# Attention stage: where the queue of GpSimd begins the reload of x, the value chunks and the z gates

## The chip, the cores and the metric

The kernel runs on one core of one Trainium2 chip. A core has TensorE (PE, matrix multiply), VectorE (DVE), ScalarE (ACT), GpSimd (POOL) and SyncE (SP). Each engine works through its own instructions in order, and engines wait for each other on semaphores. SP, ACT and POOL also begin DMA transfers; all transfers of the core share 16 DMA engines. The metric is the device time of one execution in microseconds (us), the median of several runs.

## The reference

One layer of an encoder with 2048 tokens (a grid of 32 rows by 64 columns) and 1024 features. What matters here:

```python
h = rmsnorm(x, norm_w) * (1 + scale) + shift
proj = h @ w_in + b_in              # q, k, v, z of 8 attention heads; inputs of 4 mLSTM heads
na_out = neighbourhood_attention(na_q, na_k, na_v, rpb) * silu(na_z)   # window of 8 rows by 16 columns
ml_out = groupnorm(mlstm_forward + mlstm_backward, gated) * silu(ml_z)
y = concatenate([na_out, ml_out]) @ w_out
x = x + gate * y
out = rmsnorm(x, final_norm_w)
```

All inputs and the output are float32.

## The kernel before, in words

Phase 1 computes the projections and the mLSTM branch. Phase 2, the part that the change touches, is the neighbourhood attention, the output projection, the residual and the final norm. It begins at about 1005 us of the span.

**Patches, units, slots.** The 2048 queries are cut into 16 patches of 128 (8 grid rows by 16 columns). A patch has four units of two heads each. A *slot* (`slot(m)`) takes the two units of its number (`new`) through scores and softmax and the two of the slot before (`old`) through the values. So each patch has a **first slot** (m even) and a **second slot** (m odd); a slot takes about 10 to 11 us. In a slot PE first does the scores of the new units (L1341), then the values of the old ones (L1384), then four groups of transposes of the new probabilities (`turned`, L1369, n = 0 to 3). Between these groups `pump` puts matmuls of the output projection (L1429) of an earlier patch, so that PE has work while DVE and ACT do the softmax. Where DVE is late with a softmax, PE stands at the next transpose, since its order is fixed when the program is written.

**Softmax.** DVE adds the table of biases (`tab`) to the scores and takes a minimum (L1349), ACT takes the exponential (L1350), DVE normalises (L1361). Tables are loaded by SP (`load_tab`, L1313), where the next unit that needs another one follows: issued in one slot, right behind the exponential that read the old table, and read at the start of the next slot.

**What POOL does here.** In phase 2 POOL computes almost nothing; it begins DMA transfers, strictly in program order, and a transfer whose semaphores are not there yet holds up all behind it:

- value chunks `v` of the next patch (L1269), six buffers; each waits until PE has read the buffer's last chunk. They are begun by `loads(n)`: the unit with i = 1 of a patch begins one, the unit with i = 2 one, the unit with i = 3 the rest;
- the z gates of the next patch (L1279, tiles `zs` and `gtile` in turn), begun by `loads(n)` at i = 2; they wait until DVE has split the gated output that lies in that tile (L1404);
- the mLSTM half of the mixed rows (L1286, `load_m`, tiles `whi_a` and `wlo_a`);
- the store of a finished patch (L1472), which waits for DVE's last multiply (L1471);
- the reload of the rows of x (L1297, `load_x`) for the patch after the next one, 512 KB into the buffer that the store has just read. It waits for that store to land. The rows are needed where DVE adds the projection to x (L1434).

**When a store and a reload are called.** `step()` is called behind the second and the fourth group of transposes of each slot and takes one entry of the list `todo`. The store puts two entries behind itself:

```python
nc.gpsimd.dma_start(to, x)
if nxt not in (None, last_b):
    self.todo += [lambda: None, lambda: load_x(nxt)]
```

The store comes behind the fourth group of a second slot; so the empty entry is taken at the next step, behind the second group of the first slot of the next patch, and the reload behind its fourth group. In front of all groups of a slot stands `for n in new: loads(n)`. That POOL gets to these instructions early or late is decided by their semaphores and by what stands ahead of them in POOL's order, not by PE's place in the slot.

Of the kernel before, what the change touches and what calls it, by code (L numbers as in the profile page):

```python
# [62 lines left out]
class Kernel:  # L63
# [1142 lines left out]
    def phase2(self):  # L1206
# [45 lines left out]
        def load_q(i):  # L1252
            if 2 * i >= NU:
                return
            b, c0 = units[2 * i][0], min(units[2 * i][1], units[2 * i + 1][1])
            (nc.gpsimd, nc.gpsimd, nc.scalar, nc.sync)[min(i, 3)].dma_start(qs[i % 3].bitcast(F32), self.d_qna[:, c0 // 2, b].rearrange("e p c q -> p e c q"))

        def load_v(b, most=4, queue=nc.gpsimd):

            pr, pc, nr, nkc, nk, rpc, nch = geo[b]  # L1260
            up = pc % 2 == 0
            for i in reversed(range(nch)) if up else range(nch):
                r0 = PR_R0[pr] + i * rpc
                key = (pc, r0) if nkc == 32 else (b, r0)
                if key not in chunks and most:
                    most -= 1
                    n = rpc if nkc == 32 else min(rpc, nr - i * rpc)
                    chunks[key] = p.tile([P, 512], F32, tag="v", bufs=6, name=f"v_{b}_{i}")
                    queue.dma_start(chunks[key][: n * nkc, :], vg[r0 : r0 + n, PC_C0[pc] : PC_C0[pc] + nkc, :])  # L1269
            L[b]["v"] = [  # L1270
                (chunks.get(((pc if nkc == 32 else b), PR_R0[pr] + i * rpc)), min(rpc, nr - i * rpc) * nkc) for i in range(nch)
            ]
# [5 lines left out]
        def load_z(b, queue=nc.gpsimd):  # L1278
            queue.dma_start(zs[pos[b] % 2], self.d_zna[b])  # L1279
# [8 lines left out]
        def load_x(b):  # L1288
            pr, pc = divmod(b, 4)
            src = xg[8 * pr : 8 * pr + 8, 16 * pc : 16 * pc + 16, :]  # L1290
            if b == last_b:
                L[b]["x"] = [p.tile([P, 512], F32, tag="v", bufs=6, name=f"xr_{b}_{i}") for i in range(2)]
                for i, x in enumerate(L[b]["x"]):
                    nc.gpsimd.dma_start(x, src[:, :, 512 * i : 512 * i + 512])
                return
            x = flat(self.raw.tile([P, 4, 256], F32, tag=f"raw{pos[b] % 2}", name=f"xr_{b}"))
            nc.gpsimd.dma_start(x, src)  # L1297
            L[b]["x"] = [x[:, 512 * i : 512 * i + 512] for i in range(2)]
            L[b]["row"] = x
# [56 lines left out]
        def normalised(u):  # L1356
            nk = geo[units[u][0]][4]
            pts, sums = U[u]
            nc.vector.reciprocal(sums, sums)
            for j in range(2):  # L1360
                nc.vector.tensor_scalar(pts[j][:, :nk], pts[j][:, :nk], sums[:, j : j + 1], None, ALU.mult)  # L1361
            U[u] = pts
# [11 lines left out]
        def values(pair):  # L1374
            po = pO.tile([P, 2, P], F32, tag="pO", name=f"pO_{pair[0]}")
            for u in pair:
                b, ct = units[u]
                nch = geo[b][6]
                pt = U.pop(u)
                for i in range(nch):  # L1380
                    v, n = L[b]["v"][i]
                    for j in range(2):
                        h = 2 * ct + j
                        nc.tensor.matmul(po[j * HD : (j + 1) * HD, ct % 2, :], v[:n, h * HD : (h + 1) * HD], pt[j][:n, i, :], start=(i == 0), stop=(i == nch - 1))  # L1384
            return po
# [12 lines left out]
        def mix_high(b, half):  # L1398
            nc.scalar.activation(mix_parts(b)[0][:, 4 * half : 4 * half + 4, :], mix_source(b, half), AF.Copy)  # L1399

        def mix_low(b, half):
            split.add((b, half))
            hi, lo = (part[:, 4 * half : 4 * half + 4, :] for part in mix_parts(b))
            nc.vector.tensor_tensor(lo, mix_source(b, half), hi.bitcast(F32), ALU.subtract)  # L1404

        def outproj(b):
# [9 lines left out]
            nxt = after.get(after.get(b))  # L1416
# [52 lines left out]
            def store():  # L1469
                x = lb["row"]  # L1470
                nc.vector.scalar_tensor_tensor(x, x, rst, fnw[0].bitcast(F32), ALU.mult, ALU.mult)  # L1471
                nc.gpsimd.dma_start(to, x)  # L1472
                if nxt not in (None, last_b):
                    self.todo += [lambda: None, lambda: load_x(nxt)]

            if end:
                self.between.append(scale)
# [34 lines left out]
        def loads(n):  # L1512
            b, ct = units[n]
            i = n % 4
            nb = after.get(b)
            if b == last_b and i == 1:
                load_x(b)
            if nb is not None and i:
                load_v(nb, 1 if i < 3 else 4)
                if i == 2 and b != b0:  # L1520
                    load_z(nb)

        self.flush()
        while self.left > 108 or self.jobs:
            self.pump(3)
            self.job()
            self.flush()
        self.between, self.squares = [], []

        def step():  # L1530
            if self.between:
# [7 lines left out]
        def mixed(b, half):  # L1539
            mix_high(b, half)  # L1540
            mix_low(b, half)
            if half:
                self.queue.append(outproj(b))

        def slot(m):
            new = (2 * m, 2 * m + 1) if 2 * m < NU else ()
            old = (2 * m - 2, 2 * m - 1) if m else ()
            if m:
                load_q(m + 2)
            if new:  # L1550
                scores(new)
            if old:
                po = values(old)
            if new:
                normalised(new[0])
            if old:
                gated(old, po)
            if new:
                normalised(new[1])
            b = units[old[0]][0] if m > 2 and old[0] % 4 == 2 else None  # L1560
            for n in new:
                loads(n)
            if not new:
                mixed(b, 1)
                mixed(b, 0)
                for _ in range(2):
                    self.pump(12)
                    finish()
                    step()
                return  # L1570
            fills = [8, 7, 7, 7, 7] if m < 3 else [6, 5, 5, 4, 4]
            for n in range(-1, 4):
                if n >= 0:
                    turned(new[n // 2], n % 2)
                    if n % 2:
                        step()
                    finish()
                    if n in (1, 2) and b is not None:
                        mixed(b, n % 2)
                for fn in extra.pop((m, n), ()):  # L1580
                    fn()
                self.pump(fills[n + 1])
            if m == 2:
                self.pump(max(0, self.left) + 1)
                self.owed = 0
                mixed(b0, 1)
                mixed(b0, 0)
# [90 lines left out]
```

## Time and profile before

| what | number |
|---|---|
| time, median of 3 runs (lowest, highest) | 1388.98 us (1385.2 to 1394.62) |
| the profiled execution's own time | 1390.2 us |
| its span (first to last instruction) | 1388.4 us |
| PE busy | 1299.3 us, 94% of the span |
| DVE / ACT / POOL busy | 792.7 / 531.3 / 284.5 us |
| mean granted TensorE clock of the profiled execution | 0.981 of full speed |
| DMA queues, share of 16 engines over the span: SP's / POOL's / ACT's | 48.7% / 11.0% / 9.9% |
| store of a patch from issue to landing, 512 KB, 15 times | 6.8 us median |
| reload of x from issue to landing, 512 KB, 15 times | 9.4 us median |

How to read it: the rows of a timeline give an instruction's start in us from the start of the span, its duration, the engine, the line of the kernel, the operation, the tiles (written <- read), and in brackets how long the engine stood idle before it and what ended that. "DMA share" is the part of the 16 DMA engines' time in which they moved packets. q0 is the queue of the transfers that POOL begins, q1 that of SP's.

### The profile page before, as it was taken

Reading aid. Unit: us, or ns where it says so; the run is one execution under the profiler, and the core shown is the slowest. Engines: PE = TensorE matmul, PEld = TensorE weight load, DVE = VectorE, ACT = ScalarE, POOL = GpSimd, SP = SyncE. Lnnn points to the kernel's source line nnn. Section 1 sums busy time; section 2 is a strip of 40 time slices with the busy share of each in tenths; the row PEclk is TensorE's granted clock in tenths of the full one; section 3 lists DMA queues with packets and bytes.
Section 4 is the critical chain, followed back from the end, with each engine's and each line's share of the span. In section 5 each row is a group of like instructions: output and inputs, shape, how many; then the busy total and the mean of one; then the engine's idle time right before and its main releaser. Section 6 shows DMA issues by size and latency. Waiting matters only on the chain.

```text
span 1388.4 us, 23353 instructions
## 1 busy us (share of the span) xinstructions
PE 1299.3 (94%) x8204; PEld 1111.8 (80%) x8204; DVE 792.7 (57%) x2428; ACT 531.3 (38%) x1123; POOL 284.5 (20%) x306
## 2 busy tenths in 40 slices
PE   3989998998999999999999998999999999899996
PEld 2989998998887777888878876778877777778775
DVE  6683423211355569246767876867737666657664
ACT  4642334523222223213323322323346555555552
POOL 4453222424101010001213001212202211111121
PEclk9999999999999999999999999899999999999998
DMA  9799448768457685554676787646689986666971
GB/s 327 226 296 209 123 116 222 199 189 200 121 115 206 148 192 159 163 168 139 190 215 203 233 238 259 178 135 180 174 255 248 206 214 180 174 173 175 211 180 46
DMA packets 243271, 263.28 MB, mean 190 GB/s; under 512 B 31814, under 2 KB 200006, under 8 KB 243154
## 3 DMA queue, kind: packets, MB, share of 16 engines
q1 hardware_dynamic: 151774, 186.18, 48.7%
q0 software_dynamic: 20496, 36.21, 11.0%
q10 hardware_dynamic: 70884, 39.40, 9.9%
q8 instruction: 65, 1.06, 0.3%
q14 instruction: 52, 0.43, 0.1%
HBM read 177.18 MB, written 92.72 MB: 194 GB/s over the span
## 4 chain that ended last, share of the span: by engine, by line
PE 46%; DMA 9%; DVE 5%; issue 3%; ACT 1%; POOL 1%; ACTq 0%; SPq 0%; DVEq 0%; POOLq 0%
PE pq L866 18%; PE y L1429 10%; DMA tab<-d_t 4%; PE pT L1369 3%; PE pO L1384 3%; DMA kv<-d_ck 2%; PE pS L1341 2%; PE pc L430 2%; PE pc L429 2%; PE pc L431 2%; PE pi L1090 2%; PE px L1088 1%; PE dc L1036 1%; DVE pbuf L1349 1%; DMA d_mix<-zt 1%
## 5 line engine op out<-in xcount | busy, mean ns | idle before, releaser
L866 PE MATMUL pq<-hhi,whi_a 128*128 128x512 f32 x512 | 208.5, 407 | 1.9 <-DVE qst L901 1.1
L866 PE MATMUL pq<-hlo,whi_a 128*128 128x512 f32 x512 | 208.7, 408 | 0.0
L866 PE MATMUL pq<-hhi,wlo_a 128*128 128x512 f32 x512 | 208.1, 406 | 0.0
L866 PEld LDWEIGHTS pq<-hhi,whi_a 128*128 128x128 f32 x512 | 97.2, 190 | 19.5 <-issue 1.5
L866 PEld LDWEIGHTS pq<-hhi,wlo_a 128*128 128x128 f32 x512 | 97.3, 190 | 16.6
L866 PEld LDWEIGHTS pq<-hlo,whi_a 128*128 128x128 f32 x512 | 97.1, 190 | 16.7 <-issue 0.5
L1371 ACT ACTIVATE pt<-pT 96x384 f32<-96x384 f32 (+3 forms) x128 | 65.9, 515 | 85.9 <-PE pT L1369 82.7
L1350 ACT ACTIVATE pbuf<-pbuf,mn 128x480 f32<-128x480 f32 (+5 forms) x128 | 76.1, 596 | 57.3 <-DVE mn L1349 57.1
L1429 PE MATMUL y<-hhi,wlo_a 128*128 128x512 f32 (+1 forms) x272 | 91.4, 402 | 0.2 <-ACT y L1436 0.2
L1429 PE MATMUL y<-hhi,whi_a 128*128 128x512 f32 x256 | 90.6, 415 | 0.5 <-ACT whi_a L1399 0.5
L1349 DVE CUSTOM_DVE_ANT_0 pbuf<-pS,tab 128x480 f32<-128x480 f32 (+5 forms) x128 | 63.1, 539 | 45.6 <-PE pS L1341 33.6
L840 POOL TENSOR_TENSOR wlo_a<-rawq,whi_a 128x1024 fp32r<-128x1024 f32 x20 | 48.4, 2420 | 170.5 <-ACT whi_a L839 145.2
L429 PE MATMUL pvo<-whi_b,hhi 128*128 128x256 f32 x256 | 75.5, 295 | 5.7 <-DVE stvo L499 5.7
L1112 POOL TENSOR_TENSOR hm<-hm,ck 128x128 f32<-128x128 f32 x64 | 26.4, 412 | 259.5 <-DVE hm L1111 184.8
L1369 PE MATMUL pT<-ident,pbuf 128*128 128x128 f32 (+2 forms) x416 | 67.4, 275 | 12.2 <-DVE pbuf L1361 10.5
L1369 PEld LDWEIGHTS pT<-ident,pbuf 128*128 128x128 f32 (+2 forms) x416 | 50.6, 137 | 34.7 <-issue 14.5
L1093 ACT ACTIVATE num<-px,gtile 128x129 f32<-128x129 f32 x120 | 38.2, 365 | 104.9 <-PE px L1088 85.9
L431 PE MATMUL pvo<-whi_b,hlo 128*128 128x256 f32 x256 | 74.3, 290 | 0.0
L430 PE MATMUL pvo<-wlo_b,hhi 128*128 128x256 f32 x256 | 74.2, 290 | 0.0
L1020 DVE TENSOR_SCALAR wv<-kv,gtile 128x129 f32<-128x129 f32 x120 | 37.7, 322 | 62.5 <-DMA kv<-d_ck 31.8
L714 ACT ACTIVATE dec<-dec,gtile 128x128 f32<-128x128 f32 x128 | 42.0, 392 | 71.4 <-POOL dec L710 62.3
L499 DVE TENSOR_TENSOR stvo<-pvo,brow 128x256 f32<-128x256 f32 x64 | 26.5, 420 | 74.9 <-PE pvo L431 61.0
(295 smaller groups left out, 3447.5 us busy)
## 6 DMA issues: line engine op xcount, KB each, us to landing
ck<-d_ck SPq DMA_DIRECT2D x64, 384.5 KB
kv<-d_ck SPq DMA_DIRECT2D x120, 128.5 KB
rawq<-in_w_main_dram SPq DMA_DIRECT2D x28, 512.0 KB
raw<-in_w_main_dram SPq DMA_DIRECT2D x20, 512.0 KB
d_ck<-stvo SPq DMA_DIRECT2D x16, 514.0 KB
x<-in_x_dram SPq DMA_DIRECT2D x16, 512.0 KB
wada<-in_w_ada_dram SPq DMA_DIRECT2D x32, 256.0 KB
dec<-d_mneg SPq DMA_DIRECT2D x32, 256.0 KB
```

Source lines behind the costliest of these rows:

```text
L429: nc.tensor.matmul(ps, lhi(k), rhi(k), start=(k == 0), stop=False)
L430: nc.tensor.matmul(ps, lhi(k), rlo(k), start=False, stop=False)
L431: nc.tensor.matmul(ps, llo(k), rhi(k), start=False, stop=(k == KT - 1))
L714: nc.scalar.activation(t[:, d, o, :], t[:, d, o, :], AF.Exp, bias=self.cols["g"][:, d, h, c : c + 1])
L840: nc.gpsimd.tensor_tensor(lo[:, :, cs], raw, hi[:, :, cs].bitcast(F32), ALU.subtract)
L866: nc.tensor.matmul(patch_ps(ps) if patch else ps, w, self.htok(h, g, k, patch), start=(k == 0 and n == 0), stop=(k == KT - 1 and n == 2))
L1349: nc.vector.tensor_tensor_reduce(pt[:, :nk], ps, tabs[place[u]][j][:, :nk], 1.0, 3e38, ALU.add, ALU.min, mn)
L1350: nc.scalar.activation(pt[:, :nk], pt[:, :nk], AF.Exp, bias=mn, scale=-1.0, accum_out=sums[:, j : j + 1])
L1369: nc.tensor.transpose(ps[:cs, i, :], U[u][j][:, i * cs : (i + 1) * cs], self.ident)
L1371: nc.scalar.activation(t[:cs, :nch, :], ps[:cs, :nch, :], AF.Copy)
L1384: nc.tensor.matmul(po[j * HD : (j + 1) * HD, ct % 2, :], v[:n, h * HD : (h + 1) * HD], pt[j][:n, i, :], start=(i == 0), stop=(i == nch - 1))
L1429: nc.tensor.matmul(y, m[:, k, :], w[k][:, cs], start=(k == 4 and n == 0), stop=(k == 3 and n == 2))
```

## The change

Two things. The reload of x gets a list of its own, `reloads`, of which one entry is taken in every slot, behind the second group of transposes; its two entries (the empty one and the reload) are therefore taken in two slots that follow each other. And `loads` of the two new units are called behind the first and the third group of transposes, not in front of all groups.

```diff
@@ store(), in outproj
                 nc.gpsimd.dma_start(to, x)
                 if nxt not in (None, last_b):
-                    self.todo += [lambda: None, lambda: load_x(nxt)]
+                    self.reloads += [lambda: None, lambda: load_x(nxt)]
@@
-        self.between, self.squares = [], []
+        self.between, self.squares, self.reloads = [], [], []
@@ slot(m)
             b = units[old[0]][0] if m > 2 and old[0] % 4 == 2 else None
-            for n in new:
-                loads(n)
             if not new:
@@
                     finish()
                     if n in (1, 2) and b is not None:
                         mixed(b, n % 2)
+                    if n in (0, 2):
+                        loads(new[n // 2])
+                    if n == 1 and self.reloads:
+                        self.reloads.pop(0)()
                 for fn in extra.pop((m, n), ()):
                     fn()
```

The order of instructions on PE, DVE, ACT and SP stays as it was, row for row; only POOL's order changes. In the steady part it looks as follows, on POOL before, from the store of one patch to the store of the next (`xr` is a patch's rows of x, the number behind a name only tells buffers apart):

```order
L1472 DMA out_dram<-xr_11866 8x16x1024
L1269 DMA v_1_12303<-d_vna 128x1x512
L1286 DMA whi_a<-d_mix 128x512
L1297 DMA xr_12356<-in_x_dram 128x1x1024
L1269 DMA v_0_12418<-d_vna 128x1x512
L1279 DMA gtile<-d_zna 128x512
L1472 DMA out_dram<-xr_12117 8x16x1024
```

The same place on POOL in the changed kernel:

```order
L1472 DMA out_dram<-xr_11973 8x16x1024
L1286 DMA whi_a<-d_mix 128x512
L1269 DMA v_1_12344<-d_vna 128x1x512
L1269 DMA v_0_12433<-d_vna 128x1x512
L1279 DMA gtile<-d_zna 128x512
L1297 DMA xr_12459<-in_x_dram 128x1x1024
L1472 DMA out_dram<-xr_12216 8x16x1024
```

The mixed rows (L1286) have moved from behind the first value chunk to ahead of it, the second value chunk now directly follows the first, and the reload of x (L1297) has moved past the second value chunk and past the z gates.

At the start of phase 2, on POOL before (`hlo` are the output weights):

```order
L1269 DMA v_2_10566<-d_vna 120x1x512
L1316 DMA hlo_105<-d_wo 128x1024
L1297 DMA xr_10621<-in_x_dram 128x1x1024
L1316 DMA hlo_105<-d_wo 128x1024 x3
L1269 DMA v_1_10707<-d_vna 120x1x512
L1279 DMA zs<-d_zna 128x512
L1269 DMA v_0_10710<-d_vna 120x1x512
L1286 DMA wlo_a<-d_mix 128x512
L1297 DMA xr_10756<-in_x_dram 128x1x1024
```

And there in the changed kernel:

```order
L1316 DMA hlo_105<-d_wo 128x1024
L1269 DMA v_2_10617<-d_vna 120x1x512
L1297 DMA xr_10621<-in_x_dram 128x1x1024
L1316 DMA hlo_105<-d_wo 128x1024 x3
L1286 DMA wlo_a<-d_mix 128x512
L1269 DMA v_1_10722<-d_vna 120x1x512
L1279 DMA zs<-d_zna 128x512
L1269 DMA v_0_10752<-d_vna 120x1x512
L1297 DMA xr_10756<-in_x_dram 128x1x1024
```

Here one value chunk has moved behind the first load of output weights, and the mixed rows ahead of three other loads. The first two reloads of x (which `extra` calls, not `reloads`) stay where they were.

## The prediction

> **What bounds the kernel now.** I read the page's head first, then the busy time by stretch, then PE's waits, then the chain of work that ended last.
>
> ```profile
> span 1388.4 us, 23353 instructions
> PE 1299.3 (94%) x8204; PEld 1111.8 (80%) x8204; DVE 792.7 (57%) x2428; ACT 531.3 (38%) x1123; POOL 284.5 (20%) x306
> ```
>
> PE is the bound over the whole span; the change touches the attention stage alone. The next rows give its stretches (us from the start; length; busy time and instructions of PE, PE's weight loads, DVE, ACT and POOL; granted clock, DMA share, GB/s).
>
> ```profile
> 1084.00:1128.00 44.00, 40.45 (x298) 31.70 (x297) 25.96 (x91) 22.82 (x62) 8.42 (x14) 1.00 0.93 208
> 1128.00:1193.00 65.00, 65.00 (x494) 51.52 (x492) 42.99 (x136) 36.60 (x91) 11.75 (x19) 1.00 0.66 178
> 1193.00:1214.00 21.00, 17.09 (x120) 13.54 (x117) 12.83 (x45) 10.35 (x28) 3.15 (x5) 0.92 0.86 206
> 1281.00:1350.00 69.00, 68.09 (x508) 53.61 (x506) 44.20 (x153) 38.54 (x106) 15.50 (x25) 1.00 0.85 195
> ```
>
> Where the DMA engines are 66% busy PE has no gap at all; it loses time only where they are at 85% or more. What it loses, and to whom, between 1084 and 1350 us, where the change acts:
>
> ```profile
> PE pT L1369 <- DVE pbuf L1361: 8.4, 7, 3.9
> ```
>
> Seven waits, 8.4 us, each a transpose that stands for a softmax. The chain of work that ended last tells why DVE was late (start, length, what; the lines between are PE's):
>
> ```profile
> 1090.06 9.21 DMA tab<-d_t
> ...
> 1110.30 11.10 DMA tab<-d_t
> ...
> 1196.08 12.51 DMA tab<-d_t
> ```
>
> Three times the chain leaves PE for a load of a bias table. All three are issued in a first slot and read at the start of the second slot, that is, in the stretch in which POOL's queue also holds the store, a value chunk, the mixed rows, the reload of x and another chunk. Five of PE's seven waits stand in second slots:
>
> ```profile
> 1100.50 0.51 PE L1369 MATMUL pT<-ident,pbuf 128*96 128x128 f32 x3 [1.08 <-DVE pbuf L1361]
> ...
> 1122.76 0.41 PE L1369 MATMUL pT<-ident,pbuf 128*128 128x128 f32 x2 [2.12 <-DVE pbuf L1361]
> ...
> 1210.00 0.88 PE L1369 MATMUL pT<-ident,pbuf 128*128 128x128 f32 x3 [3.91 <-DVE pbuf L1361]
> ...
> 1213.26 0.71 PE L1429 MATMUL y<-hhi,wlo_a 128*128 128x512 f32 x2
> ...
> 1334.18 0.51 PE L1369 MATMUL pT<-ident,pbuf 128*120 128x128 f32 x3 [0.27 <-DVE pbuf L1361]
> ```
>
> With one of 0.45 us between the last two shown, the five sum to 1.08 + 2.12 + 3.91 + 0.45 + 0.27 = 7.83 us; the two in first slots have the rest of the 8.4, 0.6 us. The longest costs more than itself: the granted clock of its stretch is 0.92, and from the first transpose after it to the matmul behind the second group of transposes PE takes 1213.26 - 1210.00 = 3.26 us. The same sequence without a wait:
>
> ```profile
> 1186.35 0.49 PE L1369 MATMUL pT<-ident,pbuf 128*128 128x128 f32 x3
> ...
> 1188.07 0.48 PE L1429 MATMUL y<-hhi,whi_a 128*128 128x512 f32 x1
> ```
>
> takes 1.72 us, so the slower clock adds 1.5 us. **The ceiling of what the change can give is 7.8 + 1.5 = 9.3 us, 0.7%**. A measurement of this kernel can tell about 1% (14 us) from no change.
>
> **The change, part by part.** No instruction is added or removed, and PE, DVE, ACT and SP keep their order. Only POOL's order of transfers changes, and POOL computes nothing here until the last patch; so every term is a transfer that starts earlier or later, worth what it does to a waiting reader or to the 16 DMA engines. POOL's timeline of one patch:
>
> ```profile
> 1191.23 0.62 POOL L1472 DMA_DIRECT2D out_dram<-xr  x1 [5.54 <-DVE xr L1471]
> 1194.62 0.68 POOL L1269 DMA_DIRECT2D v<-d_vna  x1 [2.77 <-PE pO L1384]
> 1195.28 0.61 POOL L1286 DMA_DIRECT2D whi_a<-d_mix  x1
> 1198.25 0.60 POOL L1297 DMA_DIRECT2D xr<-in_x_dram  x1 [2.36 <-issue]
> 1198.85 0.68 POOL L1269 DMA_DIRECT2D v<-d_vna  x1
> 1202.83 0.58 POOL L1279 DMA_DIRECT2D gtile<-d_zna  x1 [3.30 <-DVE wlo_a L1404]
> ```
>
> *The reload of x* now stands behind the z gates, which wait for DVE's split. So it starts at 1202.83 + 0.58 = 1203.4, not 1198.25: 5.2 us later. That the program calls it half a slot to a slot later does not matter beyond this, since POOL was there and waiting.
>
> *The mixed rows* no longer stand behind a chunk that waits for PE: they follow the store, at 1191.9, 3.4 us earlier. *The first chunk* keeps its own wait for PE (1194.6). *The second chunk* is no longer behind the reload: it starts at about 1195.3, 3.6 us earlier. *The z gates* start when DVE lets them, as before. *The last chunk* is behind the reload, one issue (0.6 us) later. At the start of the stage one chunk falls behind the first load of output weights; its first reader is three slots on.
>
> *Is a later x late for its reader?* The tightest place is this patch:
>
> ```profile
> 1287.14 0.61 POOL L1297 DMA_DIRECT2D xr<-in_x_dram  x1 [2.90 <-ACT pt L1371]
> ...
> 1291.18 0.58 POOL L1279 DMA_DIRECT2D gtile<-d_zna  x1 [2.79 <-DVE wlo_a L1404]
> ```
> ```profile
> 1307.75 0.68 DVE L1434 TENSOR_TENSOR xr<-xr,y 128x512 f32<-128x512 f32 x1
> ```
> ```profile
> DMA to landing us min/median/max: 7.1/9.4/12.1
> ```
>
> The last row is that of the reloads from 1084 to 1345 us (12 of them). Starting at 1291.8 and with the longest landing, 12.1, the rows are there at 1291.8 + 0.6 + 12.1 = 1304.5, 3.2 us before DVE adds to them. So this costs nothing; if the landing grew by over 3 us, DVE would stand with all that is queued behind the addition, the next slot's softmax first. Value chunks and mixed rows of this stage are read one to two slots after their issue, so neither direction counts for them.
>
> *What the DMA engines do.* This is the term that decides. The two tables that came 3.05 and 0.94 us late were issued from here:
>
> ```profile
> 1193.35 3.12 SPq L1313 DMA_DIRECT2D tab<-d_t  x4
> ```
>
> and while they were awaited the queues shared the engines like this (1202 to 1208 us: packets, MB, share of 16 engines):
>
> ```profile
> q0 software_dynamic: 481, 0.91, 84.3%
> q1 hardware_dynamic: 166, 0.21, 19.5%
> ```
>
> POOL's queue held four fifths of the engines, SP's a fifth: the reload, issued at 1198.25, was in flight then. At this rate 0.91 MB take 0.843 x 6 = 5.1 us of the engines, so the reload's 0.52 MB take 2.9 us. In the changed kernel these 2.9 us come after the tables of the first slot. Against that the second chunk (0.26 MB, 1.5 us) comes 3.6 us earlier, but it was ahead of the tables' landing before too. The bounds of the gain are nothing (POOL's queue stays full all the same) and 9.3 us. I take: for the wait of 3.91 us a relief of 2.9 us, which leaves a gap of 1 us and so no slow clock, 2.9 + 1.5 = 4.4; for the waits of 1.08 and 2.12 us, where the reload was issued only after the last table, half, 1.6; of the two small ones half, 0.4. Together 6.4 us.
>
> *The tables of second slots* are now issued beside the reload. There are eight such groups, each beginning within a us of the z gates; the first of them:
>
> ```profile
> 1097.19 3.04 SPq L1313 DMA_DIRECT2D tab<-d_t  x4
> ```
>
> Each may land up to 2.9 us later. Of all DVE waits for tables only one at the start of a first slot is named so, and it is short:
>
> ```profile
> 1301.47 0.53 DVE L1349 CUSTOM_DVE_ANT_0 pbuf<-pS,tab 128x360 f32<-128x360 f32 x1 [0.63 <-DMA tab<-d_t]
> ```
>
> The bounds are nothing and 8 x 2.9 = 23 us. I take 2 us, near the lower end: in the stretches at 66% DMA share no table was waited for at all, and in the full ones the old reload, with its landing of up to 12 us, already ran into these groups.
>
> **Sum**: -6.4 + 2 = -4.4 us, against the profiled execution's 1390.2 us (1.8 us around its span) 1385.8. That execution is 1.2 us above the median of the runs, 1389.0, so the forecast is **1384.6 us**; its own range, with a gain between 0 and all 9.3 us, is 1379.6 to 1389.
>
> **The rivals.**
>
> *The queue stays as full* (no difference). Bytes and readers are the same; in the first slot the earlier second chunk and mixed rows take the place of x, and what first-slot tables gain second-slot tables pay. For it: in 1084 to 1128 us the DMA engines are 93% busy, so that a transfer put off there only meets the next one. Against it: after the move the first slot's part of POOL's queue is shorter by the reload's 0.52 MB when the last table is due, and table groups of the second slot had not been waited for. Time: 1389, within 2 us.
> The Trainium skill, "DMA: Bandwidth & Descriptors", section "Queues, rings and completion order", says that a DMA engine takes turns between the queues that have work, a packet at a time; by that rule alone a table load is slowed whenever POOL's queue is not empty, whichever transfer is in it, and this rival would be right wherever the queue does not run empty. The split of 84.3% to 19.5% agrees with turns between large packets and small ones (0.91 MB in 481 packets against 0.21 MB in 166); whether the queue runs empty earlier no row of the old kernel can show.
>
> *The reload starves the second slot's tables* (slower). One mechanism: the reload is issued at the same moment as SP's group in the second slot (at the first one the z gates come just before 1097.19, and the reload directly behind them), and its 2.9 us go straight into the start of the next first slot. It decides where such a group lands less than 2.9 us ahead of its first reader, which no view tells for groups that were not waited for. In the three stretches with DMA shares of 85% and more lie five of the eight groups; if all five came late by the whole 2.9 us and the first slots gained nothing, that is 14.5 us, 1403.5; with three of them late, 8.7 us, 1397.7. For it: the wait of 0.63 us above shows one group without margin. Against it: the old reload was in flight at the same time.
>
> *Late x* (slower): DVE stands at L1434 in the full stretches, some 3 us in three or four patches, 1398 to 1401. Against it stand the 3.2 us at the tightest place.
>
> *The change does nothing that it says*: POOL's order is different in every patch, so only its effect can be nil, which is the first rival.
>
> **How the numbers follow.** Forecast 0.55, queue stays full 0.25, starved tables 0.16, late x 0.04. The range of 8 in 10 goes from 1377 (all 9.3 us, and part of the runs' own spread, whose lowest is 3.8 us under the median) to 1398 (three groups late). Faster by over 1% would need more than the ceiling: 0.03, for the spread alone. Slower by over 1% needs the second rival with five groups or more, or late x on top: 0.08. Within 1%: 0.89.
>
> **What would show it.** In the changed profile: POOL rows in the order store, mixed rows, two chunks, z gates, x, chunk, with x 4 to 7 us later in the patch. Right: PE's waits for L1361 in second slots fall from 7.8 us to 3 or less, and no wait of over 3 us with slow matmuls behind it. Starved tables: DVE waits for `tab` at the start of first slots, and PE's waits for L1361 there. Late x: DVE waiting at L1434 for the reload. The prediction is wrong if PE waits in total grow, or if the wait at 1210 us was no effect of the order at all and comes back elsewhere.

## The result, and the profile after

The changed kernel takes **1383.29 us** (median of 13 runs, 1377.48 to 1388.67), the kernel before 1388.86 us in the same sitting (13 runs, 1385.2 to 1398.54). The ratio is 0.9952, with a 95% interval of 0.9935 to 0.997, or 6.7 us less (4.2 to 9.0); the two medians themselves are 5.6 us apart. The forecast was 1384.6 us, 4.4 us less. The profiled execution took 1385.16 us.

The head of the page of the changed kernel:

```profile
span 1383.4 us, 23357 instructions
PE 1291.3 (93%) x8204; PEld 1104.9 (80%) x8204; DVE 792.3 (57%) x2428; ACT 531.8 (38%) x1123; POOL 284.1 (21%) x306
```

The same instructions on PE, in 8.0 us less busy time (1299.3 before). Most of that is not the change's doing. The attention stage alone, from the first score to the end (start and end; length; busy time of PE, its weight loads, DVE, ACT, POOL; granted clock, DMA share, GB/s), before and after:

```profile
1015.98:1388.40 372.42, 349.03 (x2532) 276.60 (x2531) 229.97 (x736) 195.85 (x498) 64.23 (x102) 0.98 0.73 186
```
```profile
1015.21:1383.35 368.14, 347.22 (x2532) 275.45 (x2531) 230.51 (x736) 195.73 (x498) 64.35 (x102) 0.99 0.75 189
```

It is 4.3 us shorter, 1.8 us of which are busy time. The other 6.2 us of busy time lie ahead of the first score, where nothing was changed. The stretches that answer to those of before, in the same columns:

```profile
1084.00:1126.00 42.00, 40.98 (x303) 32.51 (x302) 26.64 (x91) 22.59 (x62) 8.67 (x14) 1.00 0.91 213
1126.00:1191.00 65.00, 65.00 (x492) 51.36 (x492) 43.19 (x136) 36.66 (x91) 12.15 (x20) 1.00 0.72 187
1191.00:1211.00 20.00, 17.79 (x135) 14.04 (x131) 13.50 (x45) 10.71 (x29) 2.62 (x5) 1.00 0.97 205
1276.00:1345.00 69.00, 67.47 (x504) 53.21 (x500) 43.99 (x153) 38.35 (x106) 15.29 (x25) 1.00 0.82 199
```

The third stretch is the one to look at: its granted clock is 1.00 now and was 0.92, and its DMA share rose from 0.86 to 0.97. The last one got worse: PE had 0.9 us of gaps in 69 us, now 1.5. PE's waits for the softmax from 1084 to 1345 us, which were 8.4 us in seven:

```profile
PE pT L1369 <- DVE pbuf L1361: 4.8, 4, 2.2
```

And the waits themselves, in PE's timeline from 1064 us on, with the scores that begin the slots around the longest:

```profile
1071.30 0.52 PE L1369 MATMUL pT<-ident,pbuf 128*120 128x128 f32 x3 [1.81 <-DVE pbuf L1361]
...
1110.99 0.52 PE L1369 MATMUL pT<-ident,pbuf 128*128 128x128 f32 x3 [1.02 <-DVE pbuf L1361]
...
1190.06 0.80 PE L1341 MATMUL pS<-hlo,qs 64*128 64x384 f32 x6
...
1206.48 0.52 PE L1369 MATMUL pT<-ident,pbuf 128*128 128x128 f32 x3 [2.21 <-DVE pbuf L1361]
...
1208.25 0.71 PE L1429 MATMUL y<-hhi,wlo_a 128*128 128x512 f32 x2
...
1212.09 0.94 PE L1341 MATMUL pS<-hlo,qs 64*128 64x480 f32 x6
...
1289.93 0.51 PE L1369 MATMUL pT<-ident,pbuf 128*96 128x128 f32 x3 [0.92 <-DVE pbuf L1361]
...
1310.11 0.52 PE L1369 MATMUL pT<-ident,pbuf 128*120 128x128 f32 x3 [0.60 <-DVE pbuf L1361]
```

Counting slots from 0, the wait of 3.91 us stood in slot 17, and here it is 2.21 us. Behind it the sequence to the second group's matmul takes 1208.25 - 1206.48 = 1.77 us, at full clock, where it took 3.26. The waits of 1.08 and 2.12 us (slots 7 and 9) are gone. New or longer are 1.81 us in slot 4, 1.02 in slot 8 (0.34 before) and 0.92 in slot 25 (nothing before).

POOL in that patch, and where SP's group of tables and DVE's reader of it stand (POOL's timeline, then SP's and DVE's rows):

```profile
1189.44 0.61 POOL L1472 DMA_DIRECT2D out_dram<-xr  x1 [5.02 <-DVE xr L1471]
1190.43 0.58 POOL L1286 DMA_DIRECT2D whi_a<-d_mix  x1 [0.38 <-PE y L1429]
1192.75 1.43 POOL L1269 DMA_DIRECT2D v<-d_vna  x2 [1.74 <-PE pO L1384]
1200.99 0.58 POOL L1279 DMA_DIRECT2D gtile<-d_zna  x1 [6.80 <-DVE wlo_a L1404]
1201.56 0.61 POOL L1297 DMA_DIRECT2D xr<-in_x_dram  x1
```
```profile
1191.49 3.76 SPq L1313 DMA_DIRECT2D tab<-d_t  x4
```
```profile
1204.64 0.56 DVE L1349 CUSTOM_DVE_ANT_0 pbuf<-pS,tab 128x384 f32<-128x384 f32 x1 [2.30 <-DMA tab<-d_t]
```

From the store to the reload it was 7.0 us (1191.23 to 1198.25) and is 12.1 us now. The order is the forecast one, and the reload follows the z gates at once. But the table is still 2.30 us late: the store, the mixed rows and two chunks go out within 5 us around SP's group. The chain of work that ended last goes through tables five times from 1084 us on:

```profile
1099.37 10.29 DMA tab<-d_t
...
1193.72 10.75 DMA tab<-d_t
...
1268.60 8.53 DMA tab<-d_t
...
1278.82 9.55 DMA tab<-d_t
...
1299.21 9.53 DMA tab<-d_t
```

That is as often as before. The prediction counts three such pieces in the chain of before and shows them, but there are two more:

```profile
1303.37 9.60 DMA tab<-d_t
...
1324.38 8.43 DMA tab<-d_t
```

The five take 50.9 us before and 48.7 now. Before, all five tables were read in second slots (7, 9, 17, 27, 29); now the first and the third are read in first slots (8 and 24).

The landing of the reloads (1080 to 1340 us, minimum, median, maximum):

```profile
DMA to landing us min/median/max: 7.8/8.6/10.4
```

The longest is shorter than before (12.1), and DVE waits nowhere for a reloaded row at L1434: the closest lands 7 us ahead of its reader.

### The profile page after: what moved, and what is told of

The parts are those of the page before. It is cut to its first block, busy times and chain, and to the rows that moved or that the text cites. A ratio compares the mean times of both kernels' runs of the same rounds, so it can differ in the third digit from the quotient of the medians.

```text
span 1383.4 us, 23357 instructions
## 1 busy us (share of the span) xinstructions
PE 1291.3 (93%) x8204; PEld 1104.9 (80%) x8204; DVE 792.3 (57%) x2428; ACT 531.8 (38%) x1123; POOL 284.1 (21%) x306
## 3 DMA queue, kind: packets, MB, share of 16 engines
q0 software_dynamic: 20496, 36.21, 10.8%
q8 instruction: 65, 1.06, 0.3%
## 4 chain that ended last, share of the span: by engine, by line
PE 46%; DMA 11%; issue 4%; DVE 4%; POOL 1%; ACT 1%; ACTq 0%; SPq 0%; DVEq 0%; POOLq 0%
PE pq L866 19%; PE y L1429 9%; DMA tab<-d_t 4%; PE pT L1369 3%; PE pO L1384 2%; PE pS L1341 2%; PE pi L1090 2%; DMA kv<-d_ck 2%; PE px L1088 2%; PE pc L429 2%; PE pc L430 2%; PE pc L431 2%; DMA d_mix<-zt 2%; PE dc L1036 1%; DMA d_qna<-qst 1%
```

## The experiments

The theory at this point: the gain is the reload's 0.52 MB, taken out of the first slot, and nearly all of it comes from one place, slot 17. Its rivals: the moved loads do it; or the waits come and go from execution to execution, and what the two profiles differ in is chance. The runs that follow were made later, on two chips, on which the kernel before took 1377 to 1380 us at the median. So times are compared only as ratios with the kernel before of the same sitting, and profiles by the lengths of stages. One length is used throughout: **from the first score matmul of slot 16 to that of slot 18**, the stage with the long wait. In the first profile of before its ends are

```profile
1191.92 0.80 PE L1341 MATMUL pS<-hlo,qs 64*128 64x384 f32 x6
...
1217.13 0.94 PE L1341 MATMUL pS<-hlo,qs 64*128 64x480 f32 x6
```

that is 25.21 us; in that of the changed kernel 1212.09 - 1190.06 = 22.03.

### Both kernels once more

Two more profiles of the kernel before, and the changed kernel again, in 12 runs.

> The kernel before, one more profile, to see which of its waits come back. Theory 'place of the order': PE's waits in slots 7 and 9 at 1.0 to 1.2 and 1.9 to 2.2 us and that of slot 17 at 3 us or more again. Rival 'chance of the run': slot 17 is anywhere between 0.4 and 4 us, and slots 7 and 9 change as well.

> The same as the run beside it: place of the order says three waits as before; chance says that they differ between the two.

> The changed kernel once more, on the chip of the runs beside it. All theories: ratio to the kernel before 0.993 to 0.998; PE's wait at the start of slot 4 near 1.8 us, against 0.2 in the kernel before.

PE's timeline of the first of the two profiles of before, the stage and its wait:

```profile
1179.33 0.80 PE L1341 MATMUL pS<-hlo,qs 64*128 64x384 f32 x6
...
1196.73 0.88 PE L1369 MATMUL pT<-ident,pbuf 128*128 128x128 f32 x3 [3.23 <-DVE pbuf L1361]
...
1205.15 0.93 PE L1341 MATMUL pS<-hlo,qs 64*128 64x480 f32 x6
```

the wait in the second:

```profile
1190.26 0.87 PE L1369 MATMUL pT<-ident,pbuf 128*128 128x128 f32 x3 [3.51 <-DVE pbuf L1361]
```

and the stage in the changed kernel:

```profile
1171.31 0.80 PE L1341 MATMUL pS<-hlo,qs 64*128 64x384 f32 x6
...
1186.47 0.52 PE L1369 MATMUL pT<-ident,pbuf 128*128 128x128 f32 x3 [0.99 <-DVE pbuf L1361]
...
1192.09 0.94 PE L1341 MATMUL pS<-hlo,qs 64*128 64x480 f32 x6
```

The changed kernel took 1371.68 us against 1378.48, ratio 0.9964 (0.9936 to 0.9993). So the gain comes back in a second sitting. What of the waits comes back (PE's waits for the softmax by slot from slot 4 on, us; slots with less than 0.3 in all five are left out):

```
                  slot 4   7     8     9     17    25    27    slots 16 to 18
before            0.21   1.08  0.34  2.12  3.91    -   0.45      25.21
before, again     0.25     -   0.61  0.80  3.23    -     -       25.82
before, again     0.18     -   1.04    -   3.51    -   0.96      24.58
changed           1.81     -   1.02    -   2.21  0.92  0.60      22.03
changed, again    0.18     -   0.59    -   0.99  0.99    -       20.78
```

**Slot 17 is the order's doing**: over 3.2 us in three of three, with matmuls at a slow clock behind it, and 2.21 and 0.99 us after the change, at full clock. The stage is 25.2 us in the mean of three and 21.4 in the mean of two, 3.8 us less. A run further down that differs from the changed kernel only at the start of the stage waited 2.38 us there with a slow clock behind it; with it the mean of three is 22.2 and the relief 3.0 us. **Slots 7 and 9 wait in some executions of the old order only**: together 3.20, 0.80 and 0 us here. The runs below say more. Three further profiles in which the early reloads stand at their old place have 2.90, 0.38 and 3.30 us there (loads alone twice, one reload); a fourth, with extra bytes, has none. The profiles in which these reloads have moved (both of the change here, the reload alone, the start of the stage, the reload on SP's queue, the extra bytes in the new order) have 0.25 us at most. So these waits go with the old order, but not in every execution. Slot 8 stands in all five. Slot 25, a second slot, is new in both profiles of the change, 0.9 to 1.0 us. Slot 4 has 1.81 and 0.18 us in the same order.

### Each half of the change alone

The reload alone gets its list; the loads stay in front of the transposes:

```diff
-                    self.todo += [lambda: None, lambda: load_x(nxt)]
+                    self.reloads += [lambda: None, lambda: load_x(nxt)]
...
+                    if n == 1 and self.reloads:
+                        self.reloads.pop(0)()
```

> Only the reload of x moves (behind the z gates and all value chunks); loads stay in front of the transposes, as before. Theory 'relief' (the gain comes from taking the reload's 0.52 MB out of POOL's queue while the first slot's tables are awaited): nearly all of the change's gain, 5 to 8 us faster than the kernel before (ratio 0.994 to 0.997), PE's waits for L1361 in second slots at 3 to 5 us instead of 7.8. Rival 'chunk order' (the gain comes from the mixed rows and chunks that start earlier): 0 to 2 us faster.

The loads alone move; the reload stays in `todo`:

```diff
-            for n in new:
-                loads(n)
...
+                    if n in (0, 2):
+                        loads(new[n // 2])
```

> Only the loads of chunks and z gates move behind the transposes; the reload of x is called where it was before. Relief: within 2 us of the kernel before, second-slot waits 6 to 9 us, the chain leaves PE for tables at the same three places. Chunk order: 4 us faster or more.

The same kernel once more, for a second profile:

> The kernel with only the loads moved (reload in its old place), one more profile. If the mixed rows ahead of the first chunk free slot 17: its wait under 1 us again, slots 7 and 9 again at 1 and 2 us. If slot 17 is chance: it is not bound to this order and may be 2 us or more.

Against 1377.21 us of the kernel before, the reload alone took 1371.83 (0.9977, 0.9951 to 1.0002), the loads alone 1369.9 (0.9962, 0.9934 to 0.9989). The wait of slot 17 with the reload moved alone:

```profile
1192.10 0.52 PE L1369 MATMUL pT<-ident,pbuf 128*128 128x128 f32 x3 [1.17 <-DVE pbuf L1361]
```

with the loads moved alone, in the first and in the second profile:

```profile
1204.13 0.52 PE L1369 MATMUL pT<-ident,pbuf 128*128 128x128 f32 x3 [0.40 <-DVE pbuf L1361]
```
```profile
1199.24 0.52 PE L1369 MATMUL pT<-ident,pbuf 128*128 128x128 f32 x3 [0.88 <-DVE pbuf L1361]
```

The stage is 20.93, 20.20 and 20.68 us long. **Either half frees slot 17 alone**, and the two do not add. In time the loads alone are clear of no change (5.2 us, 1.5 to 9.1); the reload alone, 3.2 us (-0.3 to 6.7), is not, and stays under the 5 to 8 us expected of it. "The reload alone" is therefore too narrow a theory, and the expectation for the loads was missed.

What the halves have in common is argued, not isolated. In the one the reload is behind the z gates. In the other the mixed rows are 2.3 us ahead of the first chunk instead of behind it; but the reload, called where it was, also starts a little later against SP's group of tables. It starts 4.9, 5.1 and 5.0 us behind the group's beginning in the three profiles of before, with waits of 3.91, 3.23 and 3.51 us, and 5.7 and 5.4 us behind it with the loads moved, with waits of 0.40 and 0.88 us. So half a us at the old place may be enough. In the loads' first profile the waits of slots 7 and 9 are back, with 0.99 and 1.91 us; in the second they are nearly gone (0 and 0.38).

### One reload of thirteen

The kernel before, with only the reload moved that is called in the patch of slots 16 and 17:

```diff
-                    self.todo += [lambda: None, lambda: load_x(nxt)]
+                    (self.reloads if pos[nxt] == 7 else self.todo).extend([lambda: None, lambda: load_x(nxt)])
...
+                    if n == 1 and self.reloads:
+                        self.reloads.pop(0)()
```

> The kernel before with one single reload moved, that of the patch whose turn is at slot 16 (behind the z gates and the chunk of slot 17); the twelve others and all loads stay. Theory 'one place' (most of the change's gain is the wait at slot 17, which stood at 3.2 to 3.9 us in three profiles of the old order): the stretch from slot 16 to slot 18 takes 20 to 22.5 us instead of 24.6 to 25.8, and the time is 2 to 6 us under the kernel before. Rival 'many patches': that stretch keeps 24 us or more, or the time is within 1 us of the kernel before.

1373.8 us against 1380.41, ratio 0.9964 (0.9933 to 0.9995), the same as that of the whole change in its second sitting. The stage:

```profile
1187.42 0.80 PE L1341 MATMUL pS<-hlo,qs 64*128 64x384 f32 x6
...
1202.34 0.52 PE L1369 MATMUL pT<-ident,pbuf 128*128 128x128 f32 x3 [0.75 <-DVE pbuf L1361]
...
1207.95 0.93 PE L1341 MATMUL pS<-hlo,qs 64*128 64x480 f32 x6
```

20.53 us, down from 25.2 by 4.7. In this profile the waits of slots 7 and 9, where POOL's order is that of before, are 0.74 and 2.56 us, so that its whole attention stage is no shorter than that of before; the time of 12 runs is the better witness. A single transfer that starts later at one place explains a gain of the size that all thirteen give; that it is the whole of it the intervals can't say.

### What the reload costs at all

The reloads that the store calls are left out, and the rows of the patch before are used in their place; so this kernel leaves out 13 transfers of 0.52 MB and computes the residual from the wrong rows.

```diff
-                    self.todo += [lambda: None, lambda: load_x(nxt)]
+                    self.todo += [lambda: None, lambda: L[nxt].update(x=lb["x"], row=lb["row"])]
```

> The kernel before without the 13 reloads of x that the store calls (those patches go on with the rows that lie in the buffer, so this part of the computation is left out). Relief: second-slot waits of PE for L1361 under 1.5 us, 8 to 11 us faster than before (ratio 0.992 to 0.994), which is what the reload costs in all. Rival 'queue stays as full': store, chunks and mixed rows are enough to keep the tables late, second-slot waits 4 us or more, 2 to 5 us faster.

1367.72 us against 1377.21, ratio 0.9948 (0.9918 to 0.9979): 7.2 us (2.9 to 11.3). The stage from slot 16 to slot 18:

```profile
1183.06 0.80 PE L1341 MATMUL pS<-hlo,qs 64*128 64x384 f32 x6
...
1202.65 0.94 PE L1341 MATMUL pS<-hlo,qs 64*128 64x480 f32 x6
```

19.59 us, with no wait in it. Of 5.6 us that were to be had there (25.2 - 19.6) the change takes 3.8, on average. Of PE's other waits in second slots 0.94 us is left, in slot 27. So the reload is behind nearly all of them, and its whole price, a little under the 8 to 11 us expected, is not far above what the change gains.

### The reload on SP's queue

The changed kernel, with the reload begun by SP, behind the tables of the second slot:

```diff
-                    self.reloads += [lambda: None, lambda: load_x(nxt)]
+                    self.reloads += [lambda: None, lambda: load_x(nxt, nc.sync)]
```

> The changed kernel with the reload issued by SP, directly behind the second slot's tables in SP's own queue, not by POOL. Relief: tables of both slots are now ahead of the reload, PE's waits for L1361 after 1084 us at 2 to 4 us, 8 to 11 us faster than before. Rival 'late x': the reload lands later or holds up SP's next loads, DVE waits at L1434 or for tables of the next slot, and the time is 2 us or more above the changed kernel's.

1373.51 us, ratio 0.9979 (0.9953 to 1.0005), far from the 8 to 11 us expected. PE's waits in first slots nearly vanish (0.18 us in all; 2.83 and 0.77 in the two profiles of the change), and DVE waits for no table there, against 0.6 to 5.2 us in the profiles of the two kernels. That fits a reload which, behind the tables in one queue, doesn't delay them; it is one profile. But slot 17 still waits, and this time the clock falls behind it, as the matmul of 0.63 us shows (0.39 at full clock):

```profile
1196.97 0.52 PE L1369 MATMUL pT<-ident,pbuf 128*128 128x128 f32 x3 [2.00 <-DVE pbuf L1361]
...
1197.56 0.63 PE L1429 MATMUL y<-hlo,wlo_a 128*128 128x512 f32 x1
```

No better than the change itself.

### More bytes at the place of the reload

In both orders each of the 13 reloads is followed by an extra load of half its size (0.26 MB, into a tile that nothing reads there):

```diff
-        def load_x(b):
+        def load_x(b, more=False):
...
+            if more:
+                nc.gpsimd.dma_start(flat(m0), src[:, :, :512])
```

> The kernel before, and behind each of its 13 later reloads of x half of the same rows once more, into a tile that is free by then (0.26 MB, about 1.5 us of the DMA engines each). Relief (tables of the first slot wait for what the reload brings into the queue): PE's waits in second slots grow by 3 to 8 us over the kernel before, the time by as much. Rival 'queue stays as full': the same bytes cost as much in the order of the changed kernel (the next run).

> The changed kernel with the same additional half reloads behind its reloads. Relief: waits in second slots as in the changed kernel within 1.5 us, waits in first slots grow by 1 to 4 us; the time grows by less than half of what the same bytes add to the kernel before. Rival 'queue stays as full': it grows by as much.

In the old order 1380.68 us (1.0012 of the kernel before, 0.9976 to 1.0047), 2.2 us more by the medians than without the extra bytes; in the new order 1377.92 (0.9994, 0.9963 to 1.0025), 6.2 us more by the medians than the changed kernel of that sitting. The intervals overlap, so the two can't be told apart; but the theory wanted the larger loss in the old order, by 3 to 8 us of waits in second slots, and there they came down to 1.0 us in all. PE's waits for the softmax from 1060 to 1345 us (two lines further down in these kernels), in the old order with the extra bytes:

```profile
PE pT L1371 <- DVE pbuf L1363: 5.2, 5, 2.3
```

and in the new one:

```profile
PE pT L1371 <- DVE pbuf L1363: 7.7, 7, 2.3
```

Of the 7.7 us, 6.2 stand in first slots: with more bytes behind the z gates it is now the tables of second slots that come late. In the old order 4.3 of the 5.2 us stand in first slots as well; the extra bytes moved the waits there too: slot 17 had none, slot 18 waited 2.27 us with a slow clock behind it, and the stage from slot 18 to 24 was about 4 us longer. In that profile the reload started 5.75 us behind SP's group, later than in the three profiles of before. So the old place of the reload was not worse by its nature. The new place has little room as well; at the present size the reload just fits.

### The start of the stage

The changed kernel, with the loads of slot 2 in front of the transposes, as before:

```diff
+            if m == 2:
+                for n in new:
+                    loads(n)
...
-                    if n in (0, 2):
+                    if n in (0, 2) and m != 2:
```

> The changed kernel with one exception: in the third slot from the start of the stage, the loads stand in front of the transposes as before, so that the value chunk is again ahead of the output weights in POOL's queue. Theory 'start cost' (the chunk that fell between the loads of output weights delays the last of them, ACT's split of it, and the softmax of slot 4): PE's wait there 0.2 to 0.6 us instead of 1.8, and 1 to 2 us faster than the changed kernel. Rival 'chance of the run': the wait of 1.8 us stays or comes and goes without the chunk, and the time is that of the changed kernel.

1370.34 us, ratio 0.9946 (0.9915 to 0.9978), which can't be told from the 0.9964 of the changed kernel in the same sitting. Slot 4 waits 0.47 us in its profile; but the changed kernel's second profile had 0.18 there. Over all 14 profiles, the six with the new order at the start have 1.81, 0.18, 1.89, 1.20, 0.18 and 0.18 us in slot 4, the eight with the old order 0.57 at most. So the new order seems to cost over 1 us there in some executions; the times don't settle it. Slot 17 waited 2.38 us in this profile, again with a slow clock behind it, and its stage took 23.77 us.

## Why the prediction was right, point by point

The sign, the size and the main place of the gain came out as forecast: 4.4 us forecast, 6.7 measured (4.2 to 9.0), and in a second sitting 5.0 (1.0 to 8.8; the ratio 0.9964 of 1378.48 us). The main step, a reload that no longer runs beside the tables of the first slot, is borne out where that step alone was made: with one reload moved, slot 17 waits 0.75 us. But other terms were wrong and in part made up for each other: of the 2 us put down for the tables of second slots hardly anything reached PE, while slot 25 and, in some executions, slot 4 cost about 1 us or more that the sum did not have.

- **The ceiling, 7.8 + 1.5 = 9.3 us**: no run went past it: without any reload the kernel gains 7.2 us (2.9 to 11.3). But it was read from one execution that happened to wait much: PE's waits in second slots are 7.8, 4.0 and 4.5 us in three profiles of the kernel before.
- **Slot 17, 2.9 + 1.5 = 4.4 us**: the term that carried the forecast, and the one that is shown: 3.8 us in the stage from slot 16 to 18 (three profiles against two; 3.0 with the third of the same order there), 4.7 with that one reload moved. The load of a table that the chain of work passes there takes 12.51, 11.90 and 12.15 us in the profiles of before, 10.75 and 9.44 in those of the change, 8.97 with one reload moved. The wait was to be 1 us; it is 2.21 and 0.99, and 2.38 in that third. The price of the slow clock (1.5 us) was right for that execution; behind the waits of 3.23 and 3.51 us it was 2.8 and 1.3 us (from the wait's end to slot 18 8.42 and 6.88 us, against 5.6 at full clock). That no slow clock follows the wait of 2.21 us is luck, as the last section shows.
- **Slots 7 and 9, 1.6 us**: about right on average, and not shown by the one profile that it was read from. In the two others of the same kernel the waits sum to 0.8 us and nothing. Over the seven profiles named above with the early reloads at their old place they are 1.5 us in the mean, and at most 0.25 us where these reloads have moved.
- **The small waits of slots 27 and 29, 0.4 us**: nothing of it can be seen; slot 27 has 0.45, 0 and 0.96 us before, 0.60 and 0 after.
- **The cost at second-slot tables, 2 us**: too large for what reaches PE. Such a table is read in a first slot. Taken from the two first profiles the cost looks paid: DVE's wait for tables in first slots grew from 0.6 to 5.0 us. But the kernel before has 2.7 and 5.2 us there in its other two profiles, so that the premise, that these tables had hardly been waited for, came from one execution. PE's waits in first slots, slot 4 aside, are 0.5, 0.6 and 1.0 us before and 1.0 and 0.6 after. A late table costs DVE more than PE: DVE's whole wait for tables from 1064 to 1383 us is 9.8 us in both of the two first profiles, and all that PE waits for the softmax there, whatever the cause, is 6.6 us after the change.
- **Slot 25, not in the sum**: its wait of 0.9 to 1.0 us is new in both profiles of the change. Second slots read tables that were issued in first slots, where the sum had only relief. Why it comes no run shows.
- **The earlier chunks and mixed rows, costed at nothing**: wrong by omission. Their move is not neutral: with the reload left in its old place the loads free slot 17 (20.2 and 20.7 us in that stage). The working had given all of the relief to the reload.
- **The chunk behind the output weights at the start, nothing**: open, and probably wrong in some executions. Slot 4 waits over 1 us in three of six profiles with the new order at the start, in none of eight with the old.
- **A later x costs nothing**: right. The reload started 12.1 us behind the store instead of 7.0, landed in 10.4 us at the most, and no row was late. The forecast shift of 5.2 us was 5.1 in that patch.
- **The chain of work**: read wrongly. It passes five tables, not three; the two left out lie at slots 27 and 29, in the same kind of place, and carry small waits, so that the sum did not suffer.
- **What would show it**: POOL's order as told; no wait of over 3 us with slow matmuls. PE's waits in second slots fell from 7.8 to 3.7 us, not to 3 or less, and to 2.0 in the second profile.

The rival *the queue stays as full* was wrong on time, but its mechanism is seen: from 1191 to 1211 us the DMA engines are 97% busy now, and the tables on the chain take 8.5 to 10.8 us to land. Without any reload, too, the one table that is left on the chain takes 9.6 us. The Trainium skill's rule of turns between queues ("DMA: Bandwidth & Descriptors", section "Queues, rings and completion order") fits these landings, but no run here tests it. The packet counts that the prediction sets beside it hold many tiny packets: of the 647 from 1202 to 1208 us 274 are under 512 bytes, and the others are 221 of 4096 bytes in POOL's queue and 152 of 1 to 1.9 KB in SP's. What the order changes is by how much a table's landing misses one reader. *Starved tables* is what the kernel turns into with 0.26 MB more per reload (6.2 us lost by the medians), so this rival lay nearer than its chance of 0.16 said, in bytes if not in outcome.

What isn't located: the profiles of the attention stage, from the first score to the end, have 372.4, 369.4 and 368.3 us before and 368.1 and 365.5 after, 3.2 us less in the mean. The interval of the first timing begins at 4.2 us, that of the second at 1.0. The larger part of the difference is the stage from slot 16 to 18; whether the remainder is more of the same in executions that weren't profiled, or something else, no run settles. No version that was run is distinctly faster than the changed kernel.

## What to carry to other kernels

Where several queues share full DMA engines, look for the one transfer whose landing releases the bound engine, and move big transfers that have slack out of its flight: here one reload of 13 gave, within the noise, what the whole change gave. Before a wait is counted as the cost of an order, look for it in several profiles of both orders: of five waits that the forecast summed up, one was there each time, and two came in some executions of the old order only. A reordering that just fits leaves no room: half a reload more per patch left no gain that can be measured.

## What the runs showed of the hardware

**A slow clock follows much shorter gaps than expected, and not always.** The prediction had it only behind 3.91 us. Over the 14 profiles, PE's waits for a softmax in the attention stage (from slot 3 on) and the 512-column matmuls behind them (0.39 us at full clock, 0.63 when slow) are:

```
gap before the transpose    waits    followed by matmuls of 0.63 us
1.81 to 1.91 us               18        5
2.00 to 2.56 us                7        5
3.23 to 3.91 us                3        3
```

The stretch behind a slow one, up to the next slot, is at slot 17 1.3 to 2.8 us longer than the 5.6 us at full clock, so that a gap of 2 us can cost nearly twice its length.

**What decides is where the gap lies on a fixed grid of 3.41 us.** In each of the 14 profiles all changes of the granted clock, from the first matmuls to the end, lie whole multiples of 3.41 us apart, and behind these gaps the clock stays at half for one such step, once for two. Three places cut on this grid (columns as above: PE's busy time comes first behind the length, the granted clock is the third figure from the end): slot 17 of the kernel before, of the changed kernel, and of the run with the old order at the start.

```profile
1206.39:1209.80 3.41, 0.00 (x0) 0.00 (x0) 1.58 (x7) 1.16 (x3) 0.00 (x0) 1.00 1.02 246
1209.80:1213.22 3.42, 3.22 (x10) 2.67 (x11) 3.03 (x15) 1.36 (x5) 0.00 (x0) 0.50 0.70 233
```
```profile
1202.01:1205.42 3.41, 2.25 (x20) 1.47 (x14) 1.08 (x5) 1.21 (x5) 0.16 (x1) 1.00 1.07 251
1205.42:1208.83 3.41, 2.35 (x14) 2.02 (x15) 3.10 (x14) 2.42 (x8) 0.00 (x0) 1.00 1.05 210
```
```profile
1187.22:1190.63 3.41, 1.03 (x8) 0.58 (x6) 2.06 (x8) 1.64 (x5) 0.00 (x0) 1.00 1.06 215
1190.63:1194.05 3.42, 3.42 (x13) 2.73 (x11) 2.96 (x15) 1.10 (x4) 0.00 (x0) 0.50 1.04 168
```

In the first and the third PE is idle 3.41 and 2.38 us within one step, and the next step runs at half clock. In the second the gap of 2.21 us lies across a border, 1.16 us on one side and 1.06 on the other, and the clock stays. Over the 1273 steps at full clock between slot 2 and the last 25 us of the 14 profiles, the clock fell behind all 12 in which PE was idle for 1.88 us or more, behind one of three with 1.77 to 1.85 us, and behind none of the rest. So a gap of 2 us costs or not by where the border falls. A step at half clock takes up to 1.7 us of work; the wait of 3.23 us was followed by two such steps (6.83 us at half clock), which is why it cost 2.8 us.

The Trainium skill ("TensorE: Matmul & The Clock Gate", section "What's actually happening") states that the clock falls to half after an idle window of about 3.4 us; here it fell behind gaps of 1.9 to 2.6 us, and the measurement decides: a window need not be idle throughout, and a gap well under its length is no safe gap. The Trainium skill says in the same section that the window runs freely and is not reset when a kernel starts; the grid in these profiles agrees in its length and goes on unbroken through an execution, and what happens to it between kernels no run here shows.

**Most of the spread between executions lies outside the attention stage.** The first score of slot 0 starts between 997.1 and 1016.0 us in the 14 profiles, though the source of all that stands ahead of it is the same; from there to the end they take 361.4 to 373.8 us. And the same kernel before had medians of 1388.9, 1377.2, 1378.5 and 1380.4 us in four sittings. A change of a few us is told from such times only side by side, and from the stage that it touches.
